# Batched 64x64 matmul on one core: results stored in 1 KB runs instead of 512 B, and the last b tile loaded like the others

## The chip, the cores and the metric

The kernel runs on one core of one Trainium2 chip. The metric is the device time of one execution in microseconds (us); eight runs of the kernel before were timed, and one more execution was recorded by the hardware profiler. The core's engines are named as in the profile: PE (TensorE), DVE (VectorE), ACT (ScalarE), POOL (GpSimd) and SP (SyncE, which only issues transfers here). SBUF is the on-chip memory that the engines work from, PSUM the memory that PE writes into.

## The reference

```python
a: float32 [1024, 64, 64]
b: float32 [1024, 64, 64]
out = np.matmul(a, b)        # float32 [1024, 64, 64]
```

Each of the 1024 products is a 64x64 by 64x64 matmul. Each operand has 16.8 MB, and so has the result.

## The kernel before, in words

The work is cut into 16 tiles t of 64 products each. Two tiles make a group s of 128 products, for which a is loaded and transposed; there are eight groups.

PE multiplies 128 rows by 128 columns, and a product has only 64 of each. So b is laid out with four products side by side in the partitions (h, 4) times 32 row pairs (kp); the two rows of a pair (u) lie next to each other in a partition. The left operand is built as a block-diagonal matrix: for one set g of four products, w and u, a 128 x 128 block holds four 32 x 32 pieces of transposed a on its diagonal and zeros elsewhere. One matmul with it gives 64 columns of four products' rows of one parity w; two (u = 0 and 1) are added up in PSUM.

The steps, with their lines:

- load_a (L65): POOL issues four transfers of 256 KB (as written) for a group s; they also cast to bf16.
- load_b (L73): one transfer of a whole float32 tile of 1 MB, from SP, and from ACT for t = 1 and 3. b has four buffers, a has three.
- regroup (L79): DVE reorders a group of a in SBUF.
- transpose (L88): PE transposes 16 blocks of 128 x 128 into two PSUM tiles at_ps; DVE copies the first out (u = 0, L94) and ACT the second (u = 1, L96) into at_sb. Each copy has 1024 elements per partition.
- spread (L106): DVE copies the pieces of a tile onto the diagonals of one of the two at_bd tiles, in four copies of 32 partitions x 2048 elements. The zeros are written once (L164).
- cast (L111): ACT turns a b tile into bf16. For the last tile POOL issues four casting transfers instead (L115).
- multiply (L144): 64 matmuls of a tile, in four quarters of 16. Each quarter has a PSUM tile o_ps of its own (one bank, four buffers), and one copy of 128 partitions x 512 elements evacuates it to o_sb: by ACT (L156), in the last tile by DVE for two quarters (L154).
- store: POOL issues one transfer of 1 MB for a tile (L134), for the last tile four of 256 KB (L128). A partition of o_sb holds for each g two neighbouring rows of a result (w), so that a run in memory is 2 x 64 x 4 = 512 B. o_sb has five buffers.

The order of instructions on each engine is the order in which the code below names them (a manual schedule); the framework adds the waits. Each engine works its queue in that order. In iteration t the code names spread(t+1), at even t regroup(s+2) and load_a(s+4), then multiply(t) with its evacuation, cast(t+1), load_b(t+4), a transpose (of s+1 at even t, of s+2 at odd t) and the store of tile t-1.

Of the kernel before, what the change touches and what calls it, by code (L numbers as in the profile page):

```python
# [8 lines left out]
fp32 = mybir.dt.float32  # L9
bf16 = mybir.dt.bfloat16  # L10


@with_exitstack
def kernel(
    ctx: ExitStack,
    tc: tile.TileContext,
    a: bass.AP,
    b: bass.AP,
    out: bass.AP,
):  # L20

    nc = tc.nc
    B, M, K = a.shape
    _, _, N = b.shape  # L30
    assert (M, K, N) == (64, 64, 64) and B % 128 == 0

    n_t, n_s = B // 64, B // 128
    A_AHEAD = 3
    B_AHEAD = 4
    N_BD = 2
    HOLD = 2

    a_v = a.rearrange("(s g h) (mp v) k -> s h g mp (v k)", h=4, g=32, v=16)
    b_v = b.rearrange("(t g h) (kp u) n -> t (h kp) g (u n)", h=4, g=16, u=2)  # L40
    o_v = out.rearrange("(t g h) (mo w) n -> t (h mo) g (w n)", h=4, g=16, w=2)

    consts = ctx.enter_context(tc.tile_pool(name="consts", bufs=1))
    a_pool = ctx.enter_context(tc.tile_pool(name="a_pool", bufs=A_AHEAD))
    b_pool = ctx.enter_context(tc.tile_pool(name="b_pool", bufs=B_AHEAD))
    work = ctx.enter_context(tc.tile_pool(name="work", bufs=2))
    o_pool = ctx.enter_context(tc.tile_pool(name="o_pool", bufs=5))
    t_psum = ctx.enter_context(
        tc.tile_pool(name="t_psum", bufs=4, space=bass.MemoryType.PSUM)
    )  # L50
    o_psum = ctx.enter_context(
        tc.tile_pool(name="o_psum", bufs=4, space=bass.MemoryType.PSUM)
    )

    bd_tiles = [
        consts.tile([128, 64, 4, 32], bf16, name=f"at_bd{i}") for i in range(N_BD)
    ]
    identity = consts.tile([128, 128], bf16)
    a_tiles, b_tiles, abf_tiles, at_tiles, bbf_tiles = {}, {}, {}, {}, {}
    held = {}  # L60

    def load_a(s):
        a_sb = a_pool.tile([128, 4, 16, 64], bf16, name="a_sb")
        for h in range(4):
            nc.gpsimd.dma_start(  # L65
                out=a_sb[:, h, :, :].rearrange("p v k -> p (v k)"), in_=a_v[s, h]
            )
        a_tiles[s] = a_sb

    def load_b(t):  # L70
        b_sb = b_pool.tile([128, 16, 128], fp32, name="b_sb")
        queue = nc.scalar if t in (1, 3) else nc.sync
        queue.dma_start(out=b_sb[:], in_=b_v[t])  # L73
        b_tiles[t] = b_sb

    def regroup(s):
        a_sb = a_tiles.pop(s)
        a_bf = work.tile([128, 16, 4, 64], bf16, name="a_bf")
        nc.vector.tensor_copy(a_bf[:], a_sb[:].rearrange("p h v k -> p v h k"))  # L79
        abf_tiles[s] = a_bf  # L80
        at_tiles[s] = work.tile([128, 2, 2, 128, 8], bf16, name="at_sb")

    def transpose(s, w):
        a_cols = abf_tiles[s][:].rearrange("p v h k -> p v (h k)")
        for u in range(2):
            at_ps = t_psum.tile([128, 8, 128], bf16, name="at_ps")
            for vo in range(8):
                nc.tensor.transpose(  # L88
                    at_ps[:, vo, :], a_cols[:, 2 * vo + w, u::2], identity[:]
                )  # L90
            dst = at_tiles[s][:, w, u, :, :]
            src = at_ps[:].rearrange("p vo q -> p q vo")
            if u == 0:
                nc.vector.tensor_copy(dst, src)  # L94
            else:
                nc.scalar.copy(dst, src)  # L96

    def spread(t):
        at_v = at_tiles[t // 2][:].rearrange(
            "p w u (g mp) vo -> p (w u) g (mp vo)", g=32  # L100
        )
        half = slice(16 * (t % 2), 16 * (t % 2) + 16)
        bd_v = bd_tiles[t % N_BD][:].rearrange("p (wu g) h mo -> p wu g h mo", g=16)
        for h in range(4):
            rows = slice(32 * h, 32 * h + 32)
            nc.vector.tensor_copy(bd_v[rows, :, :, h, :], at_v[rows, :, half, :])  # L106

    def cast(t):
        b_bf = work.tile([128, 16, 128], bf16, name="b_bf")
        if t < n_t - 1:  # L110
            nc.scalar.copy(b_bf[:], b_tiles.pop(t)[:])  # L111
        else:
            for gq in range(4):
                rows = slice(4 * gq, 4 * gq + 4)
                nc.gpsimd.dma_start(out=b_bf[:, rows, :], in_=b_v[t, :, rows, :])  # L115
        bbf_tiles[t] = b_bf

    def store(t):
        for piece in held.pop(t):
            piece()  # L120

    def multiply(t):
        at_bd, b_bf = bd_tiles[t % N_BD], bbf_tiles.pop(t)
        last = t == n_t - 1
        o_sb = o_pool.tile([128, 4, 4, 2, 64], fp32, name="o_sb")

        def put(gq):
            nc.gpsimd.dma_start(  # L128
                out=o_v[t, :, 4 * gq : 4 * gq + 4, :],
                in_=o_sb[:, gq, :, :, :].rearrange("p g w n -> p (g w n)"),  # L130
            )

        def put_all():
            nc.gpsimd.dma_start(  # L134
                out=o_v[t], in_=o_sb[:].rearrange("p q g w n -> p (q g w n)")
            )

        for gq in range(4):
            o_ps = o_psum.tile([128, 4, 2, 64], fp32, name="o_ps")
            for g4 in range(4):  # L140
                g = 4 * gq + g4
                for w in range(2):
                    for u in range(2):
                        nc.tensor.matmul(  # L144
                            o_ps[:, g4, w, :],
                            at_bd[:, (2 * w + u) * 16 + g, :, :].rearrange(
                                "p h mo -> p (h mo)"
                            ),
                            b_bf[:, g, 64 * u : 64 * u + 64],
                            start=(u == 0),  # L150
                            stop=(u == 1),
                        )
            if last and gq % 2:
                nc.vector.tensor_copy(o_sb[:, gq, :, :, :], o_ps[:])  # L154
            else:
                nc.scalar.copy(o_sb[:, gq, :, :, :], o_ps[:])  # L156
        held[t] = [lambda q=q: put(q) for q in range(4)] if last else [put_all]

    with tc.manual_schedule():
        load_a(0)  # L160
        for t in range(B_AHEAD):
            load_b(t)
        for bd in bd_tiles:
            nc.vector.memset(bd[:], 0.0)  # L164
        make_identity(nc, identity)
        for s in range(1, A_AHEAD):
            load_a(s)
        regroup(0)
        transpose(0, 0)
        transpose(0, 1)  # L170
        spread(0)
        cast(0)
        regroup(1)
        load_a(A_AHEAD)
        transpose(1, 0)
        for t in range(n_t):
            s, half = t // 2, t % 2
            if t + 1 < n_t:
                spread(t + 1)
            if half == 0:  # L180
                if s + 2 < n_s:
                    regroup(s + 2)
                if s + 1 + A_AHEAD < n_s:
                    load_a(s + 1 + A_AHEAD)
            multiply(t)
            if t + 1 < n_t:
                cast(t + 1)
            if t + B_AHEAD < n_t - 1:
                load_b(t + B_AHEAD)
            if half == 0 and s + 1 < n_s:  # L190
                transpose(s + 1, 1)
            if half == 1 and s + 2 < n_s:
                transpose(s + 2, 0)
            if t >= HOLD - 1:
                store(t - HOLD + 1)
        for t in range(n_t - HOLD + 1, n_t):
            store(t)
# [30 lines left out]
```

## Time and profile before

| What | Value |
|---|---|
| Median of 8 runs | 138.71 us (138.37 to 138.91) |
| The profiled execution, its own time | 138.86 us |
| Its span, first to last instruction | 137.1 us |
| Busy: PE, DVE, ACT, POOL | 60.5, 83.5, 77.1, 46.1 us |
| Transfer queue of POOL (q0): packets, MB written, share of 16 engines | 11120, 25.69, 70.2% |
| Transfer queue of SP (q1) | 6864, 13.63, 28.3% |
| HBM traffic over the span | 33.55 MB read, 16.78 MB written: 367 GB/s |
| First multiplication of a tile starts, last store is issued | 28.9 us, 129.0 us |

The page divides the span into 40 slices; a digit is the busy share of a slice in tenths, and 9 stands for 90% or more. In the rows of groups the figures behind the bar are busy us, mean ns of one instruction, and then the idle time of the engine just before these instructions with what ended most of it. In the timeline a row has the start, the length in us, the engine and line, and in brackets the idle time ahead of it and what ended that. A store counts as landed when its completion is signalled: those of 1 MB took 21.1 us from issue at the median, the four small ones at the end 6.7 us.

### The profile page before, as it was taken

The page shows a single profiled execution, that of the slowest core. Times are in us where ns is not written, and L with a number is a line of the kernel's source. Part 1 is how long each engine was busy: PE and PEld are TensorE (multiplying, and loading weights), DVE is VectorE, ACT ScalarE, POOL GpSimd, SP SyncE. Part 2 cuts the span into 40 slices and gives each one's busy share as a digit, 9 for nine tenths or more (in the row PEclk, how much of TensorE's full clock was granted, in tenths as well). Part 3 has the DMA queues.
Part 4 walks back from the last instruction along what each step waited for, and adds up shares of the span by engine and source line. Part 5 has one row for each costly group of instructions (what it writes and reads, how often), then busy time and mean ns, then how long its engine had stood idle before and what let it go on. Part 6 is the DMA issues. An engine that isn't in the chain of part 4 may idle for free.

```text
span 137.1 us, 2992 instructions
## 1 busy us (share of the span) xinstructions
PE 60.5 (44%) x1280; PEld 58.3 (43%) x1280; DVE 83.5 (61%) x92; ACT 77.1 (56%) x96; POOL 46.1 (34%) x61
## 2 busy tenths in 40 slices
PE   0000064097844774480475707680096609068200
PEld 0000063096844774470475607580096609067100
DVE  5770066979699999999297704994067807901200
ACT  1030007248999999926967088830979667465100
POOL 6811141455234604541132534300303110843800
PEclk9999999758999999999686865899658965558965
DMA  2999999999999999999999999999999999999993
GB/s 79 296 304 310 304 278 260 208 243 273 246 246 298 371 280 271 338 379 360 278 270 357 383 344 271 280 374 378 382 385 377 384 382 385 376 234 303 268 280 109
DMA packets 19053, 41.61 MB, mean 304 GB/s; under 512 B 3168, under 2 KB 3168, under 8 KB 19040
## 3 DMA queue, kind: packets, MB, share of 16 engines
q0 software_dynamic: 11120, 25.69, 70.2%
q1 hardware_dynamic: 6864, 13.63, 28.3%
q10 hardware_dynamic: 1056, 2.10, 4.1%
q8 instruction: 10, 0.16, 0.5%
q14 instruction: 3, 0.02, 0.0%
HBM read 33.55 MB, written 16.78 MB: 367 GB/s over the span
## 4 chain that ended last, share of the span: by engine, by line
DMA 70%; POOL 8%; issue 6%; SPq 6%; ACT 2%; PE 2%; POOLq 1%; ACTq 0%
DMA a_sb<-in_a_dram 37%; DMA b_sb<-in_b_dram 17%; DMA out_dram<-o_sb 16%; SPq L73 6%; POOL a_sb L65 3%; POOL b_bf L115 2%; PE o_ps L144 2%; POOL out_dram L134 2%; POOL out_dram L128 1%; ACT b_bf L111 1%; ACT o_sb L156 1%; POOLq L223 1%; POOL identity masks.py:199 0%; POOL identity masks.py:197 0%; POOLq L128 0%
## 5 line engine op out<-in xcount | busy, mean ns | idle before, releaser
L144 PE MATMUL o_ps<-b_bf,at_bd 128*128 128x64 bf16 x1024 | 43.2, 213 | 43.6 <-ACT b_bf L111 42.9
L144 PEld LDWEIGHTS <-at_bd 128*128 128x128 bf16 x1024 | 42.2, 112 | 45.4 <-issue 37.4
L106 DVE COPY at_bd<-at_sb 32x2048 bf16<-32x2048 bf16 x64 | 46.1, 720 | 22.1 <-ACT at_sb L96 21.1
L156 ACT COPY o_sb<-o_ps 128x512 f32<-128x512 f32 x62 | 34.1, 622 | 21.9 <-DMA out_dram<-o_sb 14.4
L65 POOL DMA_DIRECT2D a_sb<-in_a_dram x32 | 20.3, 639 | 37.8 <-DMA a_sb<-in_a_dram 25.7
L111 ACT CAST b_bf<-b_sb 128x2048 bf16<-128x2048 f32 x15 | 29.2, 1944 | 5.2 <-DMA b_sb<-in_b_dram 5.2
L134 POOL DMA_DIRECT2D out_dram<-o_sb x15 | 19.1, 1272 | 38.3 <-ACT o_sb L156 19.8
L88 PE MATMUL at_ps<-identity,a_bf 128*128 128x128 bf16 x256 | 19.7, 240 | 23.7 <-DVE a_bf L79 23.7
L88 PEld LDWEIGHTS <-a_bf 128*128 128x128 bf16 x256 | 17.3, 110 | 23.9 <-DVE a_bf L79 23.9
L96 ACT COPY at_sb<-at_ps 128x1024 bf16<-128x1024 bf16 x16 | 16.9, 1055 | 17.3 <-PE at_ps L88 17.3
L94 DVE COPY at_sb<-at_ps 128x1024 bf16<-128x1024 bf16 x16 | 19.6, 1222 | 4.5 <-PE at_ps L88 4.2
L79 DVE COPY a_bf<-a_sb 128x4096 bf16<-128x4096 bf16 x8 | 10.0, 1246 | 8.8 <-DMA a_sb<-in_a_dram 8.6
L164 DVE MEMSET at_bd<- 128x4096 uint32 x2 | 6.9, 3472 | 2.5 <-PEq L212 1.7
L154 DVE COPY o_sb<-o_ps 128x512 f32<-128x512 f32 x2 | 1.4, 692 | 7.2 <-PE o_ps L144 7.2
L115 POOL DMA_DIRECT2D b_bf<-in_b_dram x4 | 3.2, 795 | 7.0 <-ACT o_sb L156 7.0
L96 ACT ACT_TABLE_LOAD x1 | 1.3, 1283 | 4.5 <-issue 4.5
L128 POOL DMA_DIRECT2D out_dram<-o_sb x4 | 3.0, 753 | 0.2 <-issue 0.2
L73 ACT MOVE_SHAPE b_sb<-in_b_dram x2 | 0.6, 318 | 1.7 <-issue 0.9
masks.py:199 POOL TENSOR_SCALAR_AFFINE_SELECT identity<-identity 128x128 bf16<-128x128 bf16 x1 | 0.3, 288 | 0.1
masks.py:197 POOL MEMSET identity<- 128x128 bf16 x1 | 0.3, 271 | 0.0
L212 POOL MEMSET const-float32-0.0<- 128x1 f32 x1 | 0.1, 99 | 0.2 <-issue 0.2
L212 POOL MEMSET const-bfloat16-1.0<- 128x1 bf16 x1 | 0.1, 101 | 0.0
(2 smaller groups left out, 0.2 us busy)
## 6 DMA issues: line engine op xcount, KB each, us to landing
out_dram<-o_sb POOLq DMA_DIRECT2D x15, 1024.0 KB, 21.1
a_sb<-in_a_dram POOLq DMA_DIRECT2D x32, 256.0 KB, 16.4
out_dram<-o_sb POOLq DMA_DIRECT2D x4, 256.0 KB, 6.7
b_bf<-in_b_dram POOLq DMA_DIRECT2D x4, 128.0 KB, 7.7
b_sb<-in_b_dram SPq DMA_DIRECT2D x13, 0.5 KB, 22.4
b_sb<-in_b_dram ACTq DMA_DIRECT2D x2, 0.5 KB, 18.5
```

The lines of the kernel that those rows point to most:

```text
L65: nc.gpsimd.dma_start(out=a_sb[:, h, :, :].rearrange("p v k -> p (v k)"), in_=a_v[s, h])
L73: queue.dma_start(out=b_sb[:], in_=b_v[t])
L79: nc.vector.tensor_copy(a_bf[:], a_sb[:].rearrange("p h v k -> p v h k"))
L88: nc.tensor.transpose(at_ps[:, vo, :], a_cols[:, 2 * vo + w, u::2], identity[:])
L94: nc.vector.tensor_copy(dst, src)
L96: nc.scalar.copy(dst, src)
L106: nc.vector.tensor_copy(bd_v[rows, :, :, h, :], at_v[rows, :, half, :])
L111: nc.scalar.copy(b_bf[:], b_tiles.pop(t)[:])
L134: nc.gpsimd.dma_start(out=o_v[t], in_=o_sb[:].rearrange("p q g w n -> p (q g w n)"))
L144: nc.tensor.matmul(o_ps[:, g4, w, :], at_bd[:, (2 * w + u) * 16 + g, :, :].rearrange("p h mo -> p (h mo)"), b_bf[:, g, 64 * u : 64 * u + 6 ...
L156: nc.scalar.copy(o_sb[:, gq, :, :, :], o_ps[:])
L164: nc.vector.memset(bd[:], 0.0)
```

## The change

The description says that the first two b loads wait for the first a load's issue; the diff has no line that does so. It has these parts:

- Results are stored in runs of 1 KB. The rows w are now four (j, 2 values, and wl, 2), and a partition of o_sb holds four neighbouring rows of a result. For this the columns of a block of at_bd are ordered (wl, h, mo) with mo 16, so that one matmul gives two row classes wl in the two halves of the PSUM partitions. Spread copies runs of 16 elements instead of 32.
- The copies from at_ps to at_sb are two of 512 elements instead of one of 1024.
- o_ps has two banks and two buffers, and holds half a tile (32 matmuls). Four copies of 64 partitions x 512 elements bring it to o_sb and move halves of partitions: in the first half of a tile by ACT, DVE, DVE, ACT, in the second half all by ACT. In the last tile a quarter is evacuated at a time, with ACT, DVE, DVE, ACT on 256 elements.
- The last b tile is loaded by SP as the others are, and cast in four parts, ACT and DVE in turn.

```diff
@@ -38,7 +38,7 @@
 
     a_v = a.rearrange("(s g h) (mp v) k -> s h g mp (v k)", h=4, g=32, v=16)
     b_v = b.rearrange("(t g h) (kp u) n -> t (h kp) g (u n)", h=4, g=16, u=2)
-    o_v = out.rearrange("(t g h) (mo w) n -> t (h mo) g (w n)", h=4, g=16, w=2)
+    o_v = out.rearrange("(t gh x) (mo w) n -> t (x mo) gh (w n)", gh=8, x=8, w=4)
 
     consts = ctx.enter_context(tc.tile_pool(name="consts", bufs=1))
     a_pool = ctx.enter_context(tc.tile_pool(name="a_pool", bufs=A_AHEAD))
@@ -49,11 +49,11 @@
         tc.tile_pool(name="t_psum", bufs=4, space=bass.MemoryType.PSUM)
     )
     o_psum = ctx.enter_context(
-        tc.tile_pool(name="o_psum", bufs=4, space=bass.MemoryType.PSUM)
+        tc.tile_pool(name="o_psum", bufs=2, space=bass.MemoryType.PSUM)
     )
 
     bd_tiles = [
-        consts.tile([128, 64, 4, 32], bf16, name=f"at_bd{i}") for i in range(N_BD)
+        consts.tile([128, 4, 16, 2, 4, 16], bf16, name=f"at_bd{i}") for i in range(N_BD)
     ]
     identity = consts.tile([128, 128], bf16)
     a_tiles, b_tiles, abf_tiles, at_tiles, bbf_tiles = {}, {}, {}, {}, {}
@@ -78,41 +78,50 @@
         a_bf = work.tile([128, 16, 4, 64], bf16, name="a_bf")
         nc.vector.tensor_copy(a_bf[:], a_sb[:].rearrange("p h v k -> p v h k"))
         abf_tiles[s] = a_bf
-        at_tiles[s] = work.tile([128, 2, 2, 128, 8], bf16, name="at_sb")
-
-    def transpose(s, w):
+        at_tiles[s] = work.tile([128, 2, 2, 32, 2, 4, 4], bf16, name="at_sb")
+
+    def transpose(s, j):
         a_cols = abf_tiles[s][:].rearrange("p v h k -> p v (h k)")
         for u in range(2):
-            at_ps = t_psum.tile([128, 8, 128], bf16, name="at_ps")
-            for vo in range(8):
-                nc.tensor.transpose(
-                    at_ps[:, vo, :], a_cols[:, 2 * vo + w, u::2], identity[:]
-                )
-            dst = at_tiles[s][:, w, u, :, :]
-            src = at_ps[:].rearrange("p vo q -> p q vo")
-            if u == 0:
-                nc.vector.tensor_copy(dst, src)
-            else:
-                nc.scalar.copy(dst, src)
+            at_ps = t_psum.tile([128, 2, 4, 128], bf16, name="at_ps")
+            for wl in range(2):
+                for vo in range(4):
+                    nc.tensor.transpose(
+                        at_ps[:, wl, vo, :],
+                        a_cols[:, 4 * vo + 2 * j + wl, u::2],
+                        identity[:],
+                    )
+            src = at_ps[:].rearrange("p wl vo (g mp) -> p wl g mp vo", mp=4)
+            for wl in range(2):
+                dst = at_tiles[s][:, j, u, :, wl, :, :]
+                if u == 0:
+                    nc.vector.tensor_copy(dst, src[:, wl])
+                else:
+                    nc.scalar.copy(dst, src[:, wl])
 
     def spread(t):
-        at_v = at_tiles[t // 2][:].rearrange(
-            "p w u (g mp) vo -> p (w u) g (mp vo)", g=32
-        )
         half = slice(16 * (t % 2), 16 * (t % 2) + 16)
-        bd_v = bd_tiles[t % N_BD][:].rearrange("p (wu g) h mo -> p wu g h mo", g=16)
+        bd = bd_tiles[t % N_BD]
         for h in range(4):
             rows = slice(32 * h, 32 * h + 32)
-            nc.vector.tensor_copy(bd_v[rows, :, :, h, :], at_v[rows, :, half, :])
+            src = at_tiles[t // 2][rows, :, :, half, :, :, :].rearrange(
+                "p j u g wl mp vo -> p (j u) (g wl) (mp vo)"
+            )
+            dst = bd[rows, :, :, :, h, :].rearrange("p ju g wl mo -> p ju (g wl) mo")
+            nc.vector.tensor_copy(dst, src)
 
     def cast(t):
         b_bf = work.tile([128, 16, 128], bf16, name="b_bf")
+        b_sb = b_tiles.pop(t)
         if t < n_t - 1:
-            nc.scalar.copy(b_bf[:], b_tiles.pop(t)[:])
+            nc.scalar.copy(b_bf[:], b_sb[:])
         else:
             for gq in range(4):
                 rows = slice(4 * gq, 4 * gq + 4)
-                nc.gpsimd.dma_start(out=b_bf[:, rows, :], in_=b_v[t, :, rows, :])
+                if gq % 2:
+                    nc.vector.tensor_copy(b_bf[:, rows, :], b_sb[:, rows, :])
+                else:
+                    nc.scalar.copy(b_bf[:, rows, :], b_sb[:, rows, :])
         bbf_tiles[t] = b_bf
 
     def store(t):
@@ -122,39 +131,48 @@
     def multiply(t):
         at_bd, b_bf = bd_tiles[t % N_BD], bbf_tiles.pop(t)
         last = t == n_t - 1
-        o_sb = o_pool.tile([128, 4, 4, 2, 64], fp32, name="o_sb")
-
-        def put(gq):
+        o_sb = o_pool.tile([128, 8, 2, 2, 64], fp32, name="o_sb")
+
+        def put(lo, n):
             nc.gpsimd.dma_start(
-                out=o_v[t, :, 4 * gq : 4 * gq + 4, :],
-                in_=o_sb[:, gq, :, :, :].rearrange("p g w n -> p (g w n)"),
+                out=o_v[t, :, lo : lo + n, :],
+                in_=o_sb[:, lo : lo + n].rearrange("p gh j wl n -> p (gh j wl n)"),
             )
 
-        def put_all():
-            nc.gpsimd.dma_start(
-                out=o_v[t], in_=o_sb[:].rearrange("p q g w n -> p (q g w n)")
-            )
-
-        for gq in range(4):
-            o_ps = o_psum.tile([128, 4, 2, 64], fp32, name="o_ps")
-            for g4 in range(4):
-                g = 4 * gq + g4
-                for w in range(2):
+        def evacuate(o_ps, gh, gl, n):
+
+            for par in range(2):
+                for wl in range(2):
+                    src = o_ps[64 * wl : 64 * wl + 64, gl : gl + n, par, :, :]
+                    dst = o_sb[64 * par : 64 * par + 64, gh : gh + n, :, wl, :]
+                    if wl == par or (gh and not last):
+                        nc.scalar.copy(dst, src)
+                    else:
+                        nc.vector.tensor_copy(dst, src)
+
+        for half in range(2):
+            o_ps = o_psum.tile([128, 4, 2, 2, 64], fp32, name="o_ps")
+            for g8 in range(8):
+                g = 8 * half + g8
+                for j in range(2):
                     for u in range(2):
                         nc.tensor.matmul(
-                            o_ps[:, g4, w, :],
-                            at_bd[:, (2 * w + u) * 16 + g, :, :].rearrange(
-                                "p h mo -> p (h mo)"
+                            o_ps[:, g8 // 2, g8 % 2, j, :],
+                            at_bd[:, 2 * j + u, g, :, :, :].rearrange(
+                                "p wl h mo -> p (wl h mo)"
                             ),
                             b_bf[:, g, 64 * u : 64 * u + 64],
                             start=(u == 0),
                             stop=(u == 1),
                         )
-            if last and gq % 2:
-                nc.vector.tensor_copy(o_sb[:, gq, :, :, :], o_ps[:])
-            else:
-                nc.scalar.copy(o_sb[:, gq, :, :, :], o_ps[:])
-        held[t] = [lambda q=q: put(q) for q in range(4)] if last else [put_all]
+                if last and g8 % 4 == 3:
+                    evacuate(o_ps, 4 * half + g8 // 4 * 2, g8 // 4 * 2, 2)
+            if not last:
+                evacuate(o_ps, 4 * half, 0, 4)
+        if last:
+            held[t] = [lambda q=q: put(2 * q, 2) for q in range(4)]
+        else:
+            held[t] = [lambda: put(0, 8)]
 
     with tc.manual_schedule():
         load_a(0)
@@ -185,7 +203,7 @@
             multiply(t)
             if t + 1 < n_t:
                 cast(t + 1)
-            if t + B_AHEAD < n_t - 1:
+            if t + B_AHEAD < n_t:
                 load_b(t + B_AHEAD)
             if half == 0 and s + 1 < n_s:
                 transpose(s + 1, 1)
```

## The prediction

> **What bounds the kernel now.** I read the page's busy slices first, then the groups, then the waits, then one steady stretch of the timeline. The slices show the transfer engines full from the second slice to the last but one, and 304 GB/s into their destinations:
>
> ```profile
> DMA  2999999999999999999999999999999999999993
> DMA packets 19053, 41.61 MB, mean 304 GB/s; under 512 B 3168, under 2 KB 3168, under 8 KB 19040
> ```
>
> So transfers set the end: sixteen tiles in some 128 us (137.1 less the first 9), 8.0 us for a tile. The groups give the prices (busy, then mean ns of one):
>
> ```profile
> L106 DVE COPY at_bd<-at_sb 32x2048 bf16<-32x2048 bf16 x64 | 46.1, 720 | 22.1 <-ACT at_sb L96 21.1
> L156 ACT COPY o_sb<-o_ps 128x512 f32<-128x512 f32 x62 | 34.1, 622 | 21.9 <-DMA out_dram<-o_sb 14.4
> L111 ACT CAST b_bf<-b_sb 128x2048 bf16<-128x2048 f32 x15 | 29.2, 1944 | 5.2 <-DMA b_sb<-in_b_dram 5.2
> L96 ACT COPY at_sb<-at_ps 128x1024 bf16<-128x1024 bf16 x16 | 16.9, 1055 | 17.3 <-PE at_ps L88 17.3
> L94 DVE COPY at_sb<-at_ps 128x1024 bf16<-128x1024 bf16 x16 | 19.6, 1222 | 4.5 <-PE at_ps L88 4.2
> L154 DVE COPY o_sb<-o_ps 128x512 f32<-128x512 f32 x2 | 1.4, 692 | 7.2 <-PE o_ps L144 7.2
> ```
>
> In the L156 row the reader sees that ACT mostly waits for stores to land: the engines are ahead. How far ahead the timeline of one tile in the busy stretch shows (start, us, engine):
>
> ```profile
> 44.24 2.03 PE L144 MATMUL o_ps<-b_bf,at_bd 128*128 128x64 bf16 x64 [1.74 <-ACT b_bf L111]
> 44.91 2.16 ACT L156 COPY o_sb<-o_ps 128x512 f32<-128x512 f32 x4
> 45.18 3.34 DVE L106 COPY at_bd<-at_sb 32x2048 bf16<-32x2048 bf16 x4
> 46.82 2.04 ACT L111 CAST b_bf<-b_sb 128x2048 bf16<-128x2048 f32 x1
> 48.62 1.16 ACT L96 COPY at_sb<-at_ps 128x1024 bf16<-128x1024 bf16 x1
> 48.91 2.03 PE L144 MATMUL o_ps<-b_bf,at_bd 128*128 128x64 bf16 x64 [1.75 <-ACT b_bf L111]
> 49.79 2.78 DVE L106 COPY at_bd<-at_sb 32x2048 bf16<-32x2048 bf16 x4
> ```
>
> A tile takes 48.91 - 44.24 = 4.67 us of engines, 3.3 under the transfers' 8.0. ACT is the slowest: four evacuations start 0.49 apart (1.97), cast to next start 1.80, at_sb copy 0.9: 4.67. This sum of start-to-start times gives the measured pace, so I use it below. Note that DVE's spread of the next tile (L106) runs beside the evacuation and holds up nothing.
>
> **What the Trainium skill says.** (1) PSUM — Partial Sum Buffer, "PSUM bank collisions raise a hardware error": ScalarE and VectorE may not touch one bank and quadrant together, so such accesses are ordered; "Engine vs sequencer instructions": their queues are strict FIFO. The trace of before agrees with order on each engine, and has no bank shared by the two. (2) TensorE: Matmul & The Clock Gate, "What's actually happening": an idle window of about 3.4 us halves the clock. The trace agrees: 64 matmuls took 2.03 us after 1.74 idle above, and 3.57 after 7.40:
>
> ```profile
> 99.63 3.57 PE L144 MATMUL o_ps<-b_bf,at_bd 128*128 128x64 bf16 x64 [7.40 <-ACT b_bf L111]
> ...
> 100.68 0.58 ACT L156 COPY o_sb<-o_ps 128x512 f32<-128x512 f32 x1 [0.18 <-PE o_ps L144]
> 101.53 0.58 ACT L156 COPY o_sb<-o_ps 128x512 f32<-128x512 f32 x1 [0.27 <-PE o_ps L144]
> ```
>
>  (3) SBUF — State Buffer, "Who interferes with whom": VectorE's fast copies and GpSimd's descriptor writing exclude each other. It fits the spread of 3.34 above against 2.78, with a store issued at 45.24.
>
> **The change, part by part.** *First b loads.* The built program puts no wait on them and leaves their order: 0.
>
> *Last b tile.* SP gets a sixteenth load behind its others, with nothing queued behind it. POOL loses four issues (3.2 us by the L115 row). The tile's transfer, whose share I can only bound, frees 0 to 2.8 us of the transfer engines (the stretch 120 to 130 us moved 269 GB/s against 381 before it); taken as 2.0. Cast in four: costed with the tail.
>
> *1 KB runs.* 32768 runs of 512 B become 16384. A 2 KB packet of the b queue takes 28.3% x 16 x 137.1 / 6864 = 90 ns, 22.6 per 512 B run. DMA: Bandwidth & Descriptors, "Why small descriptors are slow", has a fixed 3 cycles beside one per 32 B: 35 for 1 KB against 2 x 19, 8% less. Estimate: 32768 x 22.6 / 16 = 46 us of stores, 3.7 saved; bounds 0 and 3.7. POOL's issue falls from 1.17 (2048 runs; 0.75 with 512) to about 0.89 us. All of this counts only while transfers are the bound.
>
> *The copies.* ACT gets two at_sb copies of 512 for one of 1024: 0.49 + 0.59. DVE likewise 2 x 0.69 (L154's size). Each half tile is evacuated by four copies of 64 partitions x 512, as long each as today's 128 x 512 (same elements per partition): first half ACT, DVE, DVE, ACT, second half four on ACT. Spread keeps its 2048 elements in runs of 16 instead of 32: 2.78 kept. Upper bound: the half-rate mode, 1224 ns a copy (VectorE: DVE Perf Modes, "Side-by-side: where the cycles go for N=2048 bf16"); below zero is excluded, since no element goes away. Regroup's runs of 64 (1246 ns for 4096) are no faster per element than spread's 32.
>
> *The new waits decide it.* The built program orders the first half's copies as A1 (ACT, waits PE), D1 (waits A1), D2, A2 (waits D2). In DVE's queue D1 of tile t stands behind spread(t+1) and, at even t, regroup; behind it stand at_sb copies and the next spread. Behind A2 on ACT stand the second half's four copies, cast(t+1) and at_sb copies. PE waits for that cast; the spread of odd iterations waits for those at_sb copies. What ran side by side becomes a ring. From the end of D2 of one tile to the next:
>
> - Common: 0.05 hand-over, A2 0.49, four copies 1.97: the cast starts at 2.51.
> - Even t: cast ends 4.41, PE starts 4.46. PE then idles 3.5 to 4.7 us a tile, so I take the slow clock: the first 16 matmuls reach ACT after 1.05 (99.63 to 100.68) and 16 more take 0.85 (to 101.53): A1 at 6.36 to 6.95, D1 and D2 to 8.4 us. DVE's own queue (1.38 + 2.78 + 1.23 = 5.4) is ready earlier. With the fast clock: 7.75.
> - Odd t: at_sb copies start 2.51 + 1.80 = 4.31 and end 5.39; spread 5.44 to 8.22; D1 and D2 to 9.65 us. A1 was done at 7.0.
>
> A pair takes 18.05 us, 9.0 a tile: over 8.0, so transfers lose the bound and their savings are worth nothing. Waits for loads and for stores of tile t-5 (now D1's too) are covered by four iterations, 36 us, against landings of 18 to 25.
>
> Start: multiply(0) at 28.9 as now; DVE's spread(1) ends at 32.5 (two at_sb copies of 0.69), regroup(2) at 33.8, D2 at 35.2. Fourteen tiles in seven pairs: 126.4, to 161.6. Two of seven spreads on the ring meet GpSimd's lock for 0.55 each, as four of sixteen groups do in the timeline now: 1.1. Tail of the last tile: A2, copies, first cast part and PE to the first quarter's A1 4.5 us; then four quarters one after another, A, D, D, A of 256 elements with hand-overs 1.67 each: 6.7; 11.2 together. The last put: 6.0 (issue 0.75; landing 6.7 at the least today, in a full queue; bounds 4 and 8). Sum 35.2 + 126.4 + 1.1 + 11.2 + 6.0 = 179.9 us of span, and 1.8 outside it (138.86 against 137.1 in the profiled execution): 181.7. That execution lies 0.15 over the median of 138.71, within rounding here.
>
> **Rivals.**
> - *Transfers stay the bound (faster).* The place is A2's wait: if the ring took under 7.7 us a tile, transfers would set the end and the savings count: 138.9 - 3.7 - 2.0 = 133.2 us. For it: 3.3 us of spare per tile. Against: the ring's sum, whose method gives 4.67 for before.
> - *Only engine time counts.* Were D1 not behind spread, DVE would need 2.78 + 0.62 + 1.38 + 1.38 = 6.2 us a tile: 35 + 15 x 6.2 + 17 + 1.8 = 147. Against: the FIFO order.
> - *Spread loses its mode in runs of 16.* 4 x 0.54 = 2.2 more on seven odd and, after 1.6 of slack, 0.6 on seven even tiles: 20 more, 202. No row shows runs of 16; neither does the skill's condition name run length.
> - *The change leaves out the wait that it names.* True, at 0 as said.
>
> **How the numbers follow.** The ring 0.85, its own spread 166 to 195: fast clock -4.6, put and tail -4, no lock -1.1, 3% of the ring; upward the same and a slower spread of up to 0.1 a copy. Transfers 0.05, engine time 0.05, lost mode 0.05. Within 0.2% is about what a measurement can tell from no change; only the edge of the transfer case lies there: faster 0.04, same 0.01, slower 0.95. The range leaves out the three rivals and a twentieth of the ring.
>
> **What would show it.** Right: DMA slices fall to 6 to 8; DVE's D1 copies wait on ACT or stand straight behind spread, ACT's copies wait on DVE for some 1 to 3 us in each tile; multiplies alternate about 8.4 and 9.65 apart and take 3.5 us each; ACT stops waiting for stores. Wrong: DMA at 9 throughout; a pair far from 18 us; spread copies (L111 of the changed kernel) at over 0.75 us; store landing waits still there.

## The result and the profile after

The changed kernel takes 188.93 us (median of 11 runs, 188.62 to 189.13), the kernel before 138.68 us (32 runs, 138.23 to 139.10; beside the experiments its medians were 138.41 to 138.76). The ratio is 1.362, 95% interval 1.3606 to 1.3635: 50 us slower. The profiled execution took 188.73 us with a span of 186.6 us.

The page of the changed kernel, busy slices and the line under them:

```profile
DVE  6802679729851994199428952796269236813340
ACT  1200533583958394919592949385947584647330
...
DMA  4999999999999999899989387947795506060731
...
DMA packets 17469, 42.14 MB, mean 226 GB/s; under 512 B 1072, under 2 KB 1072, under 8 KB 17456
```

The row of the transfer engines, full to the end before, falls below 9 in most slices from the 23rd on and is 0 in three slices of the last fifth. The fall in packets, from 19053 to 17469, is the last b tile's part (POOL's queue has 2112 fewer, SP's 528 more); the runs of the stores don't show in this count, but in POOL's issue of a store, which went from 1.17 us to 0.89. No engine is full either: ACT and DVE swing between 9 and 1 to 5. That is the look of a chain that passes from engine to engine. The waits name its links (us in total, times, longest):

```profile
POOL out_dram L137 <- ACT o_sb L149: 116.0, 18, 9.3
...
PE o_ps L159 <- ACT b_bf L117: 70.2, 14, 6.7
ACT o_sb L149 <- DVE o_sb L151: 38.1, 19, 3.5
DVE at_bd L111 <- ACT at_sb L100: 31.4, 8, 4.7
DVE o_sb L151 <- ACT o_sb L149: 26.1, 11, 4.7
```

The second column is worth reading. Over the tiles there is about one PE wait for each cast, about one ACT wait for each D2, and in every second tile a wait of DVE's spread for the at_sb copies. POOL, which issues the stores, idles 116 us for finished results; ACT's waits for landings, 14.4 us before, are gone. The group row of spread has the size that the prediction had its doubts about:

```profile
L111 DVE COPY at_bd<-at_sb 32x2048 bf16<-32x2048 bf16 x64 | 44.2, 691 | 32.2 <-ACT at_sb L100 31.4
```

Spread's copies in runs of 16 take 691 ns, not more than the 720 of runs of 32; four of them undisturbed take 2.78 us in both. The timeline shows an odd and then an even tile, in order of time:

```profile
53.96 2.94 ACT L149 COPY o_sb<-o_ps 64x512 f32<-64x512 f32 x5 [1.46 <-DVE o_sb L151]
56.93 1.90 ACT L117 CAST b_bf<-b_sb 128x2048 bf16<-128x2048 f32 x1
...
58.85 1.07 ACT L100 COPY at_sb<-at_ps 128x512 bf16<-128x512 bf16 x2
58.88 3.57 PE L159 MATMUL o_ps<-b_bf,at_bd 128*128 128x64 bf16 x64 [4.33 <-ACT b_bf L117]
...
59.96 2.96 DVE L111 COPY at_bd<-at_sb 32x2048 bf16<-32x2048 bf16 x4 [4.53 <-ACT at_sb L100]
60.78 0.58 ACT L149 COPY o_sb<-o_ps 64x512 f32<-64x512 f32 x1 [0.86 <-PE o_ps L159]
...
62.95 1.39 DVE L151 COPY o_sb<-o_ps 64x512 f32<-64x512 f32 x2
...
64.38 2.94 ACT L149 COPY o_sb<-o_ps 64x512 f32<-64x512 f32 x5 [3.01 <-DVE o_sb L151]
```

Read it as a ring. ACT's five copies begin when D2 of the tile before ends (53.93). Cast and at_sb copies follow on ACT; the spread has waited for those at_sb copies for 4.53 us. A1 was done at 61.36, but D1 and D2 stand behind the spread in DVE's queue and start at 62.95; until they end ACT is idle for 3.01 us with its next work behind A2. This odd tile takes 64.38 - 53.96 = 10.42 us. In the next (even) tile the spread is early, PE's multiply is last, and the tile takes 8.85.

### The profile page after: what moved, and what is told of

Read it like the earlier page. It is cut to its first block, busy times and chain, and to the rows that moved or that the text cites. A ratio compares the mean times of both kernels' runs of the same rounds, so it can differ in the third digit from the quotient of the medians.

```text
span 186.6 us, 3100 instructions
## 1 busy us (share of the span) xinstructions
PE 78.6 (42%) x1280; PEld 76.4 (41%) x1280; DVE 107.5 (58%) x146; ACT 103.7 (56%) x150; POOL 38.3 (21%) x57
## 2 busy tenths in 40 slices
DMA packets 17469, 42.14 MB, mean 226 GB/s; under 512 B 1072, under 2 KB 1072, under 8 KB 17456
## 4 chain that ended last, share of the span: by engine, by line
ACT 35%; DVE 23%; issue 19%; PE 10%; DMA 7%; POOL 2%; POOLq 0%; DVEq 0%
ACT o_sb L149 17%; ACT b_bf L117 14%; DVE at_bd L111 11%; DVE o_sb L151 10%; DMA a_sb<-in_a_dram 7%; PE o_ps L159 7%; ACT at_sb L100 5%; PE at_ps L89 3%; DVE a_bf L79 2%; POOL out_dram L137 2%; POOL a_sb L65 1%; POOLq L241 0%; DVE at_sb L98 0%; POOLq L137 0%; DVEq L79 0%
## 5 line engine op out<-in xcount | busy, mean ns | idle before, releaser
L159 PE MATMUL o_ps<-b_bf,at_bd 128*128 128x64 bf16 x1024 | 56.7, 239 | 78.6 <-ACT b_bf L117 70.2
L159 PEld LDWEIGHTS <-at_bd 128*128 128x128 bf16 x1024 | 55.6, 129 | 80.4 <-issue 71.1
L149 ACT COPY o_sb<-o_ps 64x512 f32<-64x512 f32 (+1 forms) x98 | 55.1, 562 | 54.9 <-DVE o_sb L151 38.1
L111 DVE COPY at_bd<-at_sb 32x2048 bf16<-32x2048 bf16 x64 | 44.2, 691 | 32.2 <-ACT at_sb L100 31.4
L137 POOL DMA_DIRECT2D out_dram<-o_sb x19 | 18.4, 970 | 126.3 <-ACT o_sb L149 116.0
L151 DVE COPY o_sb<-o_ps 64x512 f32<-64x512 f32 (+1 forms) x38 | 24.0, 632 | 26.6 <-ACT o_sb L149 26.1
L89 PE MATMUL at_ps<-identity,a_bf 128*128 128x128 bf16 x256 | 24.5, 272 | 23.5 <-DVE a_bf L79 23.5
L89 PEld LDWEIGHTS <-a_bf 128*128 128x128 bf16 x256 | 22.0, 127 | 23.8 <-DVE a_bf L79 23.8
L100 ACT COPY at_sb<-at_ps 128x512 bf16<-128x512 bf16 x32 | 17.2, 589 | 17.2 <-PE at_ps L89 16.9
L98 DVE COPY at_sb<-at_ps 128x512 bf16<-128x512 bf16 x32 | 20.6, 686 | 5.3 <-PE at_ps L89 5.0
```

The lines of the kernel that those rows point to most:

```text
L89: nc.tensor.transpose(at_ps[:, wl, vo, :], a_cols[:, 4 * vo + 2 * j + wl, u::2], identity[:],)
L98: nc.vector.tensor_copy(dst, src[:, wl])
L100: nc.scalar.copy(dst, src[:, wl])
L137: nc.gpsimd.dma_start(out=o_v[t, :, lo : lo + n, :], in_=o_sb[:, lo : lo + n].rearrange("p gh j wl n -> p (gh j wl n)"),)
L159: nc.tensor.matmul(o_ps[:, g8 // 2, g8 % 2, j, :], at_bd[:, 2 * j + u, g, :, :, :].rearrange("p wl h mo -> p (wl h mo)"), b_bf[:, g, 64 * ...
```

## The experiments

The first theory (the ring) says that the time comes from the order of A and D copies across two queues. Its rivals: the amount of work and the shapes on ACT and DVE; the transfers.

**One: both ACT copies of the first half ahead of both DVE copies.** The same sixteen-tile work in the same shapes; only A2 no longer stands behind D1 and D2.

```diff
-            for par in range(2):
-                for wl in range(2):
...
+            order = ((0, 0), (0, 1), (1, 0), (1, 1))
+            if not last and not gh:
+                order = ((0, 0), (1, 1), (0, 1), (1, 0))
+            for par, wl in order:
```

> The changed kernel with the four copies of a tile's first half in another order: both of ScalarE's first, then both of VectorE's (the last tile as it was). The amount of work on every engine and every transfer stay the same; only ScalarE no longer waits for VectorE's copies, which stand behind the spread. Ring theory: the ring falls apart, a tile takes ScalarE's 6 x 0.59 + 1.93 + the exposed 1.9 us of the cold multiply = 7.4 us (6.8 if TensorE is warm), so about 157 us, 150 to 162. Rival, that the amount of copying or the new shapes set the pace: no change, 187 to 190. Rival, that the transfers do (stores of 1 KB runs are slower than thought): no change either.

Measured: 156.77 us (4 runs, 155.38 to 158.25), ratio to before 1.126 (1.1205 to 1.1315, without the longest of the four): 32 us of the 50 are gone. Its timeline from one multiply to the next:

```profile
58.93 3.49 PE L161 MATMUL o_ps<-b_bf,at_bd 128*128 128x64 bf16 x64 [3.03 <-ACT b_bf L117]
...
60.83 1.17 ACT L151 COPY o_sb<-o_ps 64x512 f32<-64x512 f32 x2 [0.85 <-PE o_ps L161]
...
62.45 2.35 ACT L151 COPY o_sb<-o_ps 64x512 f32<-64x512 f32 x4 [0.46 <-PE o_ps L161]
...
64.83 1.90 ACT L117 CAST b_bf<-b_sb 128x2048 bf16<-128x2048 f32 x1
...
66.78 3.57 PE L161 MATMUL o_ps<-b_bf,at_bd 128*128 128x64 bf16 x64 [3.47 <-ACT b_bf L117]
```

Outside the last tile, whose order was kept, ACT's copies no longer name DVE as what they waited for. This tile takes 7.85 us, the tiles on average 7.5, and the ring that is left is PE, evacuation, cast, PE. The transfers are at 9 until slice 30. The work is the same, so the amount of work falls as the cause of these 32 us.

**Two: multiply(t) named ahead of spread(t+1), regroup and load_a.** A and D copies still alternate, but no D copy stands behind a spread that waits for ACT.

```diff
             s, half = t // 2, t % 2
+            multiply(t)
...
-            multiply(t)
```

> The changed kernel with the spread of the next tile and the regrouping named after the tile's multiplication and its evacuation, so that VectorE's two copies stand ahead of the spread in its queue; the order ScalarE, VectorE, VectorE, ScalarE stays. Ring theory: the odd tiles lose the spread from the ring and cost as much as the even ones, 8.85 instead of 10.3 us; seven odd tiles and a first one that starts 2 us sooner give 177 us (173 to 181). If the alternation itself (not what stands in VectorE's queue) made the whole loss, nothing would change: 187 to 190. If the spread were needed so late that it now holds the next multiplication, slower: over 190.

Measured: 176.54 us (4 runs), ratio 1.2713 (1.2683 to 1.2742), 12.4 less than the changed kernel. Two multiplies of its trace, and the D copies between:

```profile
55.27 3.57 PE L159 MATMUL o_ps<-b_bf,at_bd 128*128 128x64 bf16 x64 [4.10 <-ACT b_bf L117]
...
57.79 1.39 DVE L151 COPY o_sb<-o_ps 64x512 f32<-64x512 f32 x2 [2.20 <-ACT o_sb L149]
...
64.13 3.56 PE L159 MATMUL o_ps<-b_bf,at_bd 128*128 128x64 bf16 x64 [3.58 <-ACT b_bf L117]
```

The D copies wait for A1 (2.20 us) and no longer stand behind the spread, and every tile takes the even tile's 8.86 us. A pair took 19.14 in the changed kernel, so the odd tiles lose 19.14 - 2 x 8.86 = 1.42 each, 9.9 of the 12.4 us; the first D2 ends 2.2 us sooner (32.60 for 34.84). So the spread's place in the ring is a part of the cost, and the alternation that stays here, and that run one takes out, the larger one.

**Three: the last b tile's part alone, in the kernel before.** Its load comes from SP and its cast is in four parts, as in the change.

> The kernel before with only the first part of the change: the last b tile loaded by SyncE like the others and cast in four parts by ScalarE and VectorE. The transfers set the end here, so 0 to 2.8 us less, about 136.7 us. A rival: the last tile's load queues behind the others on SyncE and lands later than GpSimd's four did, with no gain or up to 1 us lost.

Measured: 138.17 us (22 runs, 137.60 to 139.00), ratio 0.9963 (0.9946 to 0.998), 0.6 less; the forecast was 2.0. The transfer shares of the page's queues sum to 102.6% of 137.1 before and 101.1% of 137.1 here: 2.1 us of the engines were freed, as forecast. They don't all reach the end. The profiled execution, whose lines follow, took 138.89 us, one of the longest of the 22:

```profile
127.03 0.76 DVE L117 CAST b_bf<-b_sb 128x512 bf16<-128x512 f32 x2 [7.05 <-DMA b_sb<-in_b_dram]
...
127.75 3.19 PE L148 MATMUL o_ps<-b_bf,at_bd 128*128 128x64 bf16 x64 [3.20 <-ACT b_bf L119]
```

The last load lands as one tile at 127.0 and its multiply starts at 127.75, where before it started at 124.98. The last store is issued at 132.15 rather than 129.03, and the small stores then land in 4.3 us rather than 6.7. Of the kernels whose results stand where the reference has them it is the fastest of this study, 0.4% under the kernel before.

**Four: 1 KB runs alone, in the kernel before.** The store's view is changed, and nothing on the engines.

```diff
-    o_v = out.rearrange("(t g h) (mo w) n -> t (h mo) g (w n)", h=4, g=16, w=2)
+    o_v = out.rearrange("(t gh x) (mo w) n -> t (x mo) gh (w n)", gh=8, x=8, w=4)
...
-                out=o_v[t, :, 4 * gq : 4 * gq + 4, :],
+                out=o_v[t, :, 2 * gq : 2 * gq + 2, :],
```

> The kernel before with only the store's shape of the change: the same bytes of a partition go out in 8 runs of 1 KB instead of 16 of 512 B; nothing is computed anew for it, so the values land in other rows than the reference has them. It measures what the longer runs are worth where the transfers are the bound: an estimate of 3.7 us less (135 us) if the fixed cost per run counts, 0 if the transfer engines were bound by bytes.

Measured: 136.02 us (4 runs), ratio 0.9802 (0.9785 to 0.9819), 2.7 less; the forecast was 3.7. The page's row of POOL's queue (packets, MB, share):

```profile
q0 software_dynamic: 11120, 25.69, 69.9%
```

POOL's queue took 69.9% of 134.1, 93.7 us, for 96.2 before: 2.5 us. With transfers as the bound this reaches the end in full. So what the change is after is there, and worth 2.7 us, as long as the engines keep ahead.

**Five: the copies of the second half in another order.** In the changed kernel ACT's 64-partition copies start 0.59 us apart, the 128-partition ones of before 0.48. My theory was that a copy overlaps the one before it if both read the same half of the partitions.

```diff
+            order = ((0, 0), (0, 1), (1, 0), (1, 1))
+            if gh and not last:
+                order = ((1, 1), (0, 1), (0, 0), (1, 0))
...
```

> The changed kernel with ScalarE's four copies of the second half in another order, so that three of five neighbours in ScalarE's queue read the same half of the partitions as the copy ahead of them. The ring was 1.05 us a pair longer than forecast because copies of 64 partitions start 0.59 us apart and not 0.48. Theory, that a copy overlaps its forerunner's end only when both start at the same partition of their source: three gaps of five fall to 0.48, 0.33 us for a tile, 5 us in all, 184 us. Rival, that copies of half the partitions never overlap: gaps stay at 0.59 and the time at 189. If the destination's half counts, only the gaps with equal destinations fall: 3 us or less.

Measured: 185.67 us (5 runs), ratio 1.3406 (1.3376 to 1.3435), 3.3 less than the changed kernel (3.0 by the two ratios). That is between the theories, and the single instructions decide. In this order only A2 and the copy after it agree in source half and in destination half, and only these start 0.486 apart (0.592 in the changed kernel, where they agree in neither); pairs that agree in one of the two start 0.591 to 0.594 apart. So the theory of the source half falls, and these copies fit the rule that both halves have to agree. That pair also reads two different o_ps tiles, as all overlapping evacuations of before do; but the two at_sb copies read one at_ps tile, on all partitions, and start 0.48 apart. The Trainium skill ("ScalarE: Activation LUTs", "What ACT_TABLE_LOAD costs") says that ACTIVATEs in a row overlap by about 93 ns; ACT's copies overlap by 0.105 us in these traces, and not where a half changes, a condition that the page doesn't name. A second thing came along: at_sb copies start 1.80 us after the cast does, 1.92 in the changed kernel.

```profile
63.39 2.84 ACT L151 COPY o_sb<-o_ps 64x512 f32<-64x512 f32 x5 [2.71 <-DVE o_sb L153]
66.26 1.90 ACT L117 CAST b_bf<-b_sb 128x2048 bf16<-128x2048 f32 x1
68.06 1.06 ACT L100 COPY at_sb<-at_ps 128x512 bf16<-128x512 bf16 x2
```

A pair of tiles takes 18.75 us instead of the 19.09 of the first pair there: 0.1 in each tile and 0.12 in the odd one. Why the cast is overlapped here and not there, the halves don't say (cast and at_sb copies use all partitions in both); it stays open.

**Six and seven: 1 KB runs without copies that move partitions.** Can the saving of run four be had with one evacuation as before? In six (which contains three), a matmul has 64 columns instead of 128 and writes one half of the PSUM partitions, so that the evacuation stays at four ACT copies of 128 x 512; a tile has 128 matmuls instead of 64. In seven, cast(t+1) is in addition named ahead of multiply(t).

```diff
+                half = slice(64 * (g4 % 2), 64 * (g4 % 2) + 64)
...
-                            o_ps[:, g4, w, :],
+                            o_ps[half, g4 // 2, w, :],
```

> The 1 KB runs got in another way: TensorE multiplies with 64 columns at a time, 128 instead of 64 matmuls for a tile, and writes products of even and odd g into the lower and upper half of the partitions, so that evacuation stays four copies of 128 x 512 by ScalarE, with no copy that moves partitions and none by VectorE in the loop; the last b tile as in the change. If the transfers' saving is all that counts (2.7 and 0.6 us of the two parts alone) 135.4 us. Rival, that TensorE becomes the bound: with the cast behind the evacuation a tile takes 4.1 + 0.3 + 0.6 + 1.9 = 6.9 us warm, which the transfers' 7.7 hide, but 7.1 + 2.8 = 9.9 cold, which gives 28.8 + 16 x 9.9 + 8 = 195 us at the worst, some 150 with half of the tiles cold.

> As the run with 64 columns at a time, with the cast of the next b tile ahead of this tile's evacuation in ScalarE's queue, so that TensorE can go on without a wait for it: 5.2 us a tile warm. If the transfers set the end, 135.4 us (134.5 to 136.5), faster than both kernels. If TensorE stays cold, 8.6 us a tile and 28.8 + 16 x 8.6 + 8 = 174 at the worst.

Measured: six 143.35 us (6 runs), ratio 1.0344 (1.0308 to 1.038); seven 139.59 us (6 runs), ratio 1.0097 (1.0068 to 1.0127). Six lies between its two theories, and seven missed its forecast by 4. In seven the cast is out of the way, and PE waits for something else:

```profile
L152 PE MATMUL o_ps<-b_bf,at_bd 128*64 128x64 bf16 x2048 | 52.4, 209 | 32.4 <-issue 32.4
```

and in its timeline, within the last tile,

```profile
131.00 1.36 PE L152 MATMUL o_ps<-b_bf,at_bd 128*64 128x64 bf16 x33 [3.21 <-issue]
```

"issue" is idle time for which the profile shows no releaser. The stops, up to 3.2 us long, come at every 256th instruction of PE, also inside a tile. The page lists 18 packets in its instruction queue (q8) for 10 before, 16 KB each, and a stop ends 2.2 to 2.5 us after such a packet starts. That PE waits for its own instructions there is what this points to; no run took the packets away.

**Eight: run one's order, with cast(t+1) ahead of multiply(t).** If run one's remaining ring is evacuation, cast, PE, it opens here.

```diff
-            multiply(t)
             if t + 1 < n_t:
                 cast(t + 1)
+            multiply(t)
```

> The changed kernel with both of ScalarE's first copies ahead of VectorE's (157 us measured) and with the next tile's cast ahead of this tile's evacuation. What is left of the loss there should be the cast and the cold multiply on the path: without them ScalarE's own work of 6 x 0.59 + 1.9 + 1.07 = 6.5 us a tile sets the pace, 30.8 + 15 x 6.5 + about 17 of tail = 146 us (143 to 150). If the longer evacuation alone were the cause, with the cast and the multiply off the path already, no change: 157.

Measured: 142.92 us (4 runs), ratio 1.0325 (1.0302 to 1.0347), another 13.9 us less and better than forecast. Two of its slice rows, and two lines of its end:

```profile
ACT  1110038089999999999999999999999968094420
...
DMA  3999999999999999999999999999999999932832
```

```profile
123.16 1.14 ACT L124 CAST b_bf<-b_sb 128x512 bf16<-128x512 f32 x2 [3.79 <-DMA b_sb<-in_b_dram]
...
126.96 1.04 PE L161 MATMUL o_ps<-b_bf,at_bd 128*128 128x64 bf16 x16 [4.89 <-DVE o_sb L153]
```

ACT is now at 9 in 24 slices and the transfers are full until slice 35. All work of the change is in this kernel, in all its shapes, and it costs 4.5 us over its own runs of before (138.41), not 50. In the trace ACT's work of a tile takes 6.33 us (4.67 before), but the 4.5 us seem to lie in the tail. The last b tile is there at 123.1, 3.9 us sooner than in run three; from then to the end of the span pass 18.1 us, in run three 10.1. The cast of the last tile, named ahead, waits for that landing and holds up the evacuation of the tile before behind it; and the last tile's 64 multiplies, whose quarters still go A, D, D, A, stretch over 8.2 us (3.2 in run three). No run changed this tail alone.

**Nine: seven with 95 transposes at the start that nothing reads.** If seven loses its gain because a stop falls into the last tile, moving the stops should help.

> The run with 64 columns at a time and the early cast, with 95 transposes of the identity added on TensorE at the start, where it has nothing to do; nothing reads what they write. That run was 4 us over its expectation, and its TensorE stopped for 1.4 to 3.4 us at every 256th instruction of its queue, each time until 2.2 us after a packet of the instruction queue; one of these stops lies in the last tile, on the path to the end. The 190 instructions move the stops by 190, so that the one in the last tile falls ahead of its first matmul, where TensorE waits for the cast. If the stop is fetching and its place counts, 2 to 3 us less, 136.5 to 137.5 us. If the stops belong to the tiles and their waits and not to the count of instructions, they stay where they are and so does the time, 139.6 us.

Measured: 140.71 us (5 runs), ratio 1.017 (1.0149 to 1.0191). The stops kept to the same instruction counts (705, 961, 1217, to 4545), and so moved against the tiles; the last lies ahead of the last tile here. But 1.1 us were lost, not gained: PE stops there for 2.11 us, and the last tile's multiply starts when that stop ends, at 128.90 (125.75 in seven). So the stop was moved, not taken off the path. The count is confirmed, the gain from its place is not. In both runs the last b tile is there sooner than in run three (ACT casts it at 123.05 and 123.96, there at 127.08), so that the 1 KB runs seem to gain their time and PE's stops to take it back; no run shows it.

## Why the prediction was right, and where its sizes were off

The forecast was 181.7 us, the profiled execution took 188.73; by the prediction's own steps:

| Step | Forecast, us | Measured, us | Difference |
|---|---|---|---|
| End of D2 of tile 0 | 35.2 | 34.84 | -0.4 |
| Seven pairs of tiles | 7 x 18.05 = 126.4 | 168.82 - 34.84 = 133.98 | +7.6 |
| Spreads met by the lock | 1.1 | two of 2.96 for 2.78: 0.4, held in the pairs above | -1.1 |
| Tail to the last quarter's A2 | 11.2 | 182.38 - 168.82 = 13.56 | +2.4 |
| Last put | 6.0 | 186.6 - 182.38 = 4.2 | -1.8 |
| Outside the span | 1.8 | 188.73 - 186.6 = 2.1 | +0.3 |

- *Which bound.* Right: the transfers lose it (their row falls to 0), and two queues in turn on one PSUM tile set the pace. Run one shows it by 32 us, run two by 12.4, without less work. That the savings of the transfers are worth nothing here follows from their idle slices; no run took them out of this kernel. Two of the ring's waits, D1's for A1 and A2's for D2, stand between copies that read different halves of the partitions, so that the rule of one bank and quadrant, which the prediction names, doesn't ask for them; no run left them out. Odd and even tiles alternate as forecast (10.2 to 10.4 and 8.85 for 9.65 and 8.4).
- *The common part, 2.51 us, was mis-sized.* The step took start-to-start times of 128-partition copies, "as long each as today's". The length is the same (0.58), the distance is not: from A2 to the cast five starts 0.59 apart took 2.97, with the hand-over 3.00. That is 0.49 in every tile, 0.98 of the 1.09 that a pair was short; the at_sb copies' start at 1.92 after the cast instead of 1.80 is another 0.12 in odd tiles. (For the four copies the lines of the prediction give 46.82 - 44.91 = 1.91, not 1.97; its sum of 4.67 holds, since the at_sb copy takes 0.96 there.)
- *The slow clock.* Forecast as 3.57 us for 64 multiplies after idle times of 3.5 us and more; measured 3.57 after 4.33. This agrees with the Trainium skill's idle window ("TensorE: Matmul & The Clock Gate", "What's actually happening"); run eight has 2.04 us for the same 64 after waits of up to 1.8. Under the window's 3.4 us there is no sharp edge: after 3.03 us idle it is 2.89 in run eight and 3.49 in run one. The slow clock's share of the ring was not tried apart.
- *The tail's quarters, 1.67 each, were mis-sized.* They took 8.84 together for 6.7. The step left out that two quarters share one o_ps, so that PE's next quarter waits for the last copy of this one, though it writes the tile's other bank:

```profile
174.82 0.37 ACT L149 COPY o_sb<-o_ps 64x256 f32<-64x256 f32 x1 [0.92 <-DVE o_sb L151]
175.24 1.86 PE L159 MATMUL o_ps<-b_bf,at_bd 128*128 128x64 bf16 x32 [1.74 <-ACT o_sb L149]
```

- *The last put was too dear.* Its landing took 2.5 us at the median, in queues that are empty by then; the 6.7 of before was that of a full queue.
- *The savings of the transfers.* Estimated 3.7 for 1 KB runs, 2.7 by run four; 2.0 for the last b tile, 0.6 by run three, where that tile lands later. The 8% that came from the skill's cycles ("DMA: Bandwidth & Descriptors", "Why small descriptors are slow") were 2.5 us, 5% of the 46 that the prediction estimated.
- *Rivals.* Spread's mode in runs of 16 is kept (691 ns). (The prediction's aside on regroup doesn't hold: 1246 ns for 4096 elements are 0.30 ns each, spread's 695 for 2048 are 0.34.) "Only engine time counts", 147 us, is not what this kernel does, but run eight, with the ring opened, comes to 142.9. The description's wait of the first b loads is not in the program and left no mark.

The sizes that were too low (+10.3) and too high (-3.3) leave +7.0; that a third of the miss cancelled is luck.

## What to carry to other kernels

To hand part of an evacuation to a second engine is priced by what stands ahead of it in that engine's queue and by what stands behind the first engine's next copy, not by the copies' lengths: here the same work cost 50 us in one order and 4.5 us in another. Where two engines share a PSUM tile, let each do its copies in a row, and name work that others wait for (a cast of the next operand) ahead of work that waits, unless that work itself waits for a load, as the last cast of run eight. A longer store run is worth its few per cent only while transfers set the end; look first at how many us a tile of spare the engines have (3.3 here), and then at whether the new order of waits eats it.

## What was not expected of the hardware

- ACT's evacuation copies of 64 partitions overlapped the one before by 0.105 us only where both the source and the destination kept their partition half (0.486 against 0.591 us from start to start). With 0.49 us over the forecast in each of 14 tiles this was 6.9 us of the total.
- PE stopped for up to 3.5 us at every 256th instruction while the transfer engines were full, beside 16 KB packets of the instruction queue (runs seven and nine). There twice the matmuls cost more than their multiplying time: 32.4 us of such idle time in run seven.
